# Spreading a gate's weight loads over three units per head pair, and sending DRAM copies one by one between loads

## The chip, the cores and the metric

The kernel runs on one core of one Trainium2 chip. The metric is the device time of one launch in microseconds (us); lower is better. A profiled execution has one more number, its span: the time from the first to the last instruction that the hardware profiler recorded. The core has a matrix engine (PE, with its weight loads shown apart as PEld), a vector engine (DVE), a scalar engine (ACT), a general engine (POOL) and an engine that only issues transfers (SP). Sixteen DMA engines carry the transfers of all of them.

## The reference

The reference is one decoder layer with two branches side by side. Shapes: 512 tokens, width 2048, float32.

```python
cond = jax.nn.silu(c)
mod = cond @ w_ada[layer] + b_ada[layer]
shift, scale, gate = jnp.split(mod, 3, axis=-1)
u = rms_norm(h, norm_w[layer]) * (1.0 + scale[:, None, :]) + shift[:, None, :]
proj = u @ w_in[layer]
z, xbc, dt_raw, q, k, v, g = jnp.split(proj, [OFF_Z, OFF_XBC, OFF_DT, OFF_Q, OFF_K, OFF_V], axis=-1)
...   # SSD branch: conv, chunked scan, gated norm -> y_ssd (2048 wide)
...   # retention branch: 8 heads, rotary q/k, chunkwise recurrence, head norm, silu(g) -> y_ret (2048 wide)
mixed = jnp.concatenate([y_ssd, y_ret], axis=-1) @ w_out[layer]
h = h + gate[:, None, :] * mixed
return rms_norm(h, final_norm_w)
```

The gate is the last third of `cond @ w_ada`: a vector of 2048 numbers made from a 2048 x 2048 block of weights, 16 MB that are read once and used once.

## The kernel before, in words

**Number format.** Every float32 product is made of three TensorE products: an operand is split into a rounded part (`hi`, made by ACT, line 98) and the remainder (`lo`, made by DVE, line 99), and `mm3` (lines 107 to 109) adds hi x hi, hi x lo and lo x hi.

**Units.** The input projection is cut into units of 512 output columns. `unit(name, ...)` walks over the 2048 input rows in 8 steps of 256 rows. A step (`kc`) loads 512 KB into a tile `raw` (SP, line 95), splits it into `hi` and `lo`, and multiplies them into four PSUM banks named `acc` (24 matmuls of 512 columns). The last two steps are multiplied together, bank by bank. `raw` has 3 buffers, `hi` and `lo` 4 each, so SP can issue the load of a step only when the split of the load three places before has been done, and the split waits for PE when four steps lie ready. `unit` has an argument `side`: a function that is called after each step's load is traced.

**Stages.** First the conditioning and a set of units that are built up together. Then the SSD branch, groups 1 to 3, with units BC2, xs1 to xs3 and z1 to z3. Then the retention branch, four head pairs p = 0 to 3, each with a unit qk, a unit v and a unit g. `ret_a` takes the four banks of qk through the rotary step on DVE (lines 474 to 476, tiles `r` and `rt`, then POOL at line 477), `ret_b` runs the chunk recurrence (four chunks; DVE makes statistics of `po` and the new state `rnew` from `pkv`), and `ret_c` multiplies with silu(g) and writes the mixed activations to DRAM through `put_mix`. Last comes the output projection in sweeps over `w_out`, which ends in the gated residual and the norm.

**The gate.** `gate_part(n, q)` loads 512 KB of the gate's weight (block n of 4, eighth q of 8) into a buffer of the same ring `raw` (named `graw`, SP line 577) and adds two row groups into `gacc` with two DVE instructions (line 586 for the first of a block, line 588 for the rest). `gate_done(n)` loads a bias `bg` (line 593), sums over the partitions with one matmul on ones (`pg`, line 595) and adds the bias on DVE (line 596). Before the change the eight parts of block p are issued in unit v of head pair p, one after each load, and `gate_done(p)` follows that unit.

**Sums of the output weight.** The output projection uses 16 row blocks of `w_out`, each with four quarters, and sums of those quarters (T1 to T4). The sums are made by transfers alone, DRAM to DRAM. `block_sums` is called 20 times, at the end of each half stage; its calls are numbered n = 0 to 19. Call n copies the four quarters of block n into T1 to T4 (SP, line 379, 512 KB each; call 14 copies two blocks), and issues accumulating transfers for the blocks n-1, n-2 and n-3 from POOL (line 369). `behind(eng)` puts what follows behind the last instruction of that engine traced so far. The four copies of a call stand one after the other.

**Order of the work.** Each engine runs its own instructions in a fixed order. That order is set when the program is built: a planner simulates the time line and picks among the instructions whose inputs are ready, earlier ones in the program first. It moves instructions of an engine past each other where dependences allow: `bg` of head pair 0 is traced after the unit's loads, and SP issues it before the last two of them.

Of the kernel before, what the change touches and what calls it, by code (L numbers as in the profile page):

```python
# [41 lines left out]
def hybrid_block(ctx, tc, x, c_row, vecs, heads, w_mod, w_gate, b_gate, w_in, w_dt, w_out, fnw,  # L42
                 rope, dmask, xi, zeta, gdec, out):
    nc = tc.nc
    act, dve, pool, pe, sp = nc.scalar, nc.vector, nc.gpsimd, nc.tensor, nc.sync
# [8 lines left out]
    def bank(tag, name):  # L54
        return ps.tile([P, 512], F32, tag=tag, name=name)
# [30 lines left out]
    def hv(base, i):  # L86
        return half[:, base - V_SNW + i:base - V_SNW + i + 1]
# [5 lines left out]
    def load_w(src, width, eng=dve):  # L93
        raw = wp.tile([P, 2, width], F32, tag="raw", bufs=3, name="raw")
        last_load[0] = sp.dma_start(raw.rearrange("p k f -> p (k f)"), src)
        hi = wp.tile([P, 2, width], F32R, tag="hi", bufs=4, name="hi")
        lo = wp.tile([P, 2, width], F32R, tag="lo", bufs=4, name="lo")
        act.copy(hi, raw)  # L98
        eng.tensor_tensor(lo, raw, hi.bitcast(F32), ALU.subtract)  # L99
        return hi, lo  # L100
# [3 lines left out]
    def mm3(dst, a, b, first, last, more=False):  # L104

        (ah, al), (bh, bl) = a, b
        pe.matmul(dst, lhsT=ah, rhs=bh, start=first, stop=False, skip_group_check=more)  # L107
        pe.matmul(dst, lhsT=ah, rhs=bl, start=False, stop=False, skip_group_check=more)  # L108
        pe.matmul(dst, lhsT=al, rhs=bh, start=False, stop=last, skip_group_check=more)  # L109

    def unit(name, w_stationary, tag="mm", side=None):
        width = 512
        nb = width // P if w_stationary else NC
        banks = [bank(tag, f"acc{b}") for b in range(nb)]
        held = []
        for kc in range(NK // 2):
            held.append((kc, *load_w(w_in[name][kc], width)))
            if side is not None:
                side(kc)
            if kc == NK // 2 - 2:  # L120
                continue
            for b in range(nb):
                sl = slice(b * P, (b + 1) * P)
                for k, hi, lo in [(2 * c + kt, h[:, kt, :], l[:, kt, :])
                                  for c, h, l in held for kt in range(2)]:
                    if w_stationary:
                        mm3(banks[b], (hi[:, sl], lo[:, sl]), (uh[k], ul[k]),
                            k == 0, k == NK - 1)
                    else:
                        mm3(banks[b][:, :width], (uh[k][:, sl], ul[k][:, sl]), (hi, lo),  # L130
                            k == 0, k == NK - 1)
            held = []
        return banks
# [158 lines left out]
    def t2k(tag, bufs, name, shape=(P, 512)):  # L292
        pl = att1 if tag in ("bc", "xs", "zs") else att
        return pl.tile(list(shape), F32, tag=tag, bufs=bufs, name=name)
# [27 lines left out]
    B11, B12, B22, B21 = (lambda j, i=i: w_out[4 * j + i] for i in range(4))  # L322
    T1, T2, T3, T4 = (lambda j, i=i: tsum[j][i] for i in range(4))
# [9 lines left out]
    def put_mix(i, src, nw):  # L333


        pT = bank("aux", "pT")
        for c in range(NC):
            pe.transpose(pT[:, c * P:(c + 1) * P], src[c], ident)
        m = t2k("mo", 3, "m")
        act.activation(m, pT, AF.Copy, scale=nw)  # L340
        if i % 2 == 0:
            half_of["m"] = m
            return
        ma, j = half_of["m"], i // 2
        a11, a21, a12, a22 = ma[:, 0:256], ma[:, 256:], m[:, 0:256], m[:, 256:]
        g = t2k("xw", 2, "mg", (P, 2, 256))
        s3 = t2k("xd", 2, "ms", (P, 256))
        pool.tensor_tensor(s3, a11, a21, ALU.subtract)
        pool.tensor_tensor(a21, a21, a22, ALU.subtract)
        pool.tensor_tensor(g[:, 0, :], a21, a11, ALU.subtract)  # L350
        pool.tensor_tensor(g[:, 1, :], a12, g[:, 0, :], ALU.add)
        pool.dma_start(mixd["AS"][j].rearrange("p a t -> p (a t)"), ma)
        pool.dma_start(mixd["SR"][j], g)
        pool.dma_start(mixd["SA"][j][:, 0, :], s3)
        pool.dma_start(mixd["SA"][j][:, 1, :], a12)
        pool.dma_start(mixd["A22"][j // 2][:, j % 2, :], a22)
# [3 lines left out]
    def behind(eng):  # L360

        ins = next(i for i in reversed(nc.cur_bb.bb.instructions) if i.engine == eng.engine)
        return tc.issue_after(ins)

    def block_sums():


        def add(dst, src):
            pool.dma_start(dst, src, accum_op=ALU.add, max_dma_last_dim=4096)

        n = next(ticks)
        for i in range(4):
            for j in {14: (14, 15)}.get(n - i, (n - i,)):
                if not 0 <= j < 2 * QJ or n - i > 14:
                    continue
                if i == 0:
                    with behind(sp):
                        for dst, src in ((T1, B11), (T3, B12), (T2, B22), (T4, B21)):
                            sp.dma_start(dst(j), src(j))
                else:  # L380
                    with behind(pool):
                        if i == 1:
                            add(T1(j), B12(j))
                            add(T3(j), B22(j))
                        elif i == 2:
                            add(T2(j), T1(j))
                        else:
                            add(T4(j), T2(j))
# [62 lines left out]
    def silu2(pb, name, zs=None):  # L451
        th = t2k("th", 2, "th")
        act.activation(th, pb, AF.Tanh, scale=0.5)
        if zs is None:
            zs = t2k("zs", 4, name)
        dve.scalar_tensor_tensor(zs, th, 1.0, pb, ALU.add, ALU.mult)
        return zs
# [99 lines left out]
    def ret_c(p, ys, gb):  # L557
        for c in range(NC):
            gs = silu2(gb[c], f"gs{c}")
            dve.tensor_tensor(ys[c], ys[c], gs, ALU.mult)  # L560
        for i in range(4):
            put_mix(16 + 4 * p + i, [y[:, i * P:(i + 1) * P] for y in ys], hv(V_RNW, 4 * p + i))

    def take_bc(banks, g):
        for j in range(2):
            bct[("B", g + j)] = conv_silu(banks[j], 16 + g + j, "bc", 5, f"B{g + j}")
            bct[("C", g + j)] = conv_silu(banks[2 + j], 20 + g + j, "bc", 5, f"C{g + j}")

    def take_xs(banks, g):
        xst[g] = [conv_silu(b, 4 * g + i, "xs", 5, f"xs{i}") for i, b in enumerate(banks)]  # L570


    gates = {}

    def gate_part(n, q):
        raw = wp.tile([P, 2, 512], F32, tag="raw", bufs=3, name="graw")
        sp.dma_start(raw.rearrange("p k f -> p (k f)"), w_gate[8 * n + q])
        if n % 2 == 0 and q == 0:
            gates["t"] = t2k("dec", 2, "gacc", (P, HPG, P)).rearrange("p (a h) t -> p a (h t)", a=2)
        if q == 0:  # L580
            gates[n] = gates["t"][:, n % 2, :]
        gacc = gates[n]
        for kk in range(2):
            k = 2 * q + kk
            if k == 0:
                dve.tensor_scalar(gacc, raw[:, kk, :], cs[:, k:k + 1], None, ALU.mult)
            else:
                dve.scalar_tensor_tensor(gacc, raw[:, kk, :], cs[:, k:k + 1], gacc,  # L588
                                         ALU.mult, ALU.add)

    def gate_done(n):
        bg = t2k("tmp", 2, "bg")
        sp.dma_start(bg, b_gate[n * 512:(n + 1) * 512].partition_broadcast(P))
        pg = bank("aux", "pg")
        pe.matmul(pg, lhsT=ones, rhs=gates[n], start=True, stop=True)
        dve.tensor_tensor(gates[n], pg, bg, ALU.add)
# [5 lines left out]
    for b in range(4):  # L602
        z = whole("B", b)
# [63 lines left out]
    block_sums()  # L667
    for g in range(1, GROUPS):
        if g == 2:
            take_bc(unit("BC2", True), 2)  # L670
        take_xs(unit(f"xs{g}", True), g)
        ys = ssd_a(g)
        block_sums()
        zb = unit(f"z{g}", False)
        ssd_b(g, ys, [silu2(zb[c], f"zs{c}") for c in range(NC)])
        block_sums()
    for p in range(RH // 2):
        qk = unit(f"qk{p}", True)
        a = ret_a(p, qk)
        block_sums()  # L680
        vb = unit(f"v{p}", False, side=lambda kc: gate_part(p, kc))
        gate_done(p)
        ys = ret_b(p, a, vb)
        block_sums()
        gb = unit(f"g{p}", False)
        ret_c(p, ys, gb)
        block_sums()


# [229 lines left out]
```

## Time and profile before

| what | value |
|---|---|
| time of three runs | 1493.32, 1495.53, 1495.69 us (median 1495.53) |
| the profiled execution | 1496.37 us, span 1494.7 us |
| mean granted TensorE clock | 0.987 |
| PE busy | 1438.2 us, 96% of the span |
| DVE busy | 895.1 us, 60% |
| ACT busy | 540.2 us, 36% |
| POOL busy | 377.2 us, 25% |
| bytes moved by DMA | 324.09 MB, mean 217 GB/s |

The page of the profile gives busy time by engine, the span in 40 slices, the chain of work that ended last, the costliest groups of instructions, and the issues of transfers with the time from issue to landing. Two things help to read it. A matmul's recorded duration (0.39 us) is longer than the distance to the next one (0.23 us) because matmuls are pipelined, so short pauses of PE hide behind a busy share near 100%; the count of matmuls in a stretch of time shows them better. And a wait is written as "who waited <- for whom", with the idle time.

### The profile page before, as it was taken

To read this page: it belongs to the slowest core of one execution; us is meant where nothing else is said; L and a number is where in the kernel's file an instruction comes from. 1 tells how busy PE (TensorE), PEld (TensorE's weight loads), DVE (VectorE), ACT (ScalarE), POOL (GpSimd) and SP (SyncE) were. 2 spreads that over 40 slices of the span, in tenths; PEclk is the share of its full clock that TensorE was granted. 3 is DMA by queue.
4 is the path that set the end of the run, shared out by engine and by line. 5 is a ranking of instruction groups with operands and counts; after the bars stand their busy time and mean duration, and the time that the engine had idled before them with its cause. 6 is when DMAs were issued, how large, how long until landed. Compare 5 with 4: busy or idle time off the path is not lost.

```text
span 1494.7 us, 17196 instructions
## 1 busy us (share of the span) xinstructions
PE 1438.2 (96%) x6481; PEld 1174.4 (79%) x6481; DVE 895.1 (60%) x1064; ACT 540.2 (36%) x732; POOL 377.2 (25%) x440
## 2 busy tenths in 40 slices
PE   6998999899999999999999999999899999999997
PEld 4766888788888888778877888888788778888885
DVE  6899786777556654643363436433644466558585
ACT  7423353434424423121312131213232356446453
POOL 4540105576035245301340124023200200000000
PEclk9999999999999999999999999999999999999999
DMA  9887753556647748876578659664744598777755
GB/s 361 339 316 282 246 185 99 185 161 185 212 160 199 216 155 239 217 255 189 189 202 258 181 184 285 213 158 136 207 155 143 190 320 279 246 244 263 245 179 195
DMA packets 86263, 324.09 MB, mean 217 GB/s; under 512 B 11298, under 2 KB 11474, under 8 KB 81058
## 3 DMA queue, kind: packets, MB, share of 16 engines
q1 hardware_dynamic: 67858, 262.30, 51.2%
q0 software_dynamic: 17168, 58.59, 16.9%
q10 hardware_dynamic: 1152, 2.10, 0.4%
q8 instruction: 51, 0.84, 0.2%
q14 instruction: 34, 0.27, 0.1%
HBM read 304.00 MB, written 86.05 MB: 261 GB/s over the span
## 4 chain that ended last, share of the span: by engine, by line
PE 64%; DVE 13%; DMA 10%; issue 8%; POOL 3%; ACT 1%; SPq 1%; DVEq 0%; POOLq 0%; ACTq 0%
PE acc L108 13%; PE acc L107 13%; PE acc L109 13%; DMA graw<-w_gate_d 5%; DVE ada L189 4%; PE U L108 3%; PE U L109 3%; PE U L107 3%; PE W L107 2%; PE W L108 2%; PE W L109 2%; DVE gacc L588 1%; DVE lo L99 1%; PE py L428 1%; DVE ul L206 1%
## 5 line engine op out<-in xcount | busy, mean ns | idle before, releaser
L98 ACT CAST hi<-raw 128x1024 fp32r<-128x1024 f32 (+1 forms) x184 | 186.1, 1015 | 483.5 <-PE acc L109 150.6
L99 DVE TENSOR_TENSOR lo<-raw,hi 128x1024 fp32r<-128x1024 f32 (+1 forms) x166 | 210.5, 1271 | 250.0 <-ACT hi L98 249.6
L107 PE MATMUL acc<-hi,uh 128*128 128x512 f32 x704 | 278.2, 397 | 8.9 <-DVE rt L476 6.4
L108 PE MATMUL acc<-lo,uh 128*128 128x512 f32 x704 | 280.5, 398 | 1.6 <-DVE lo L99 1.5
L109 PE MATMUL acc<-hi,ul 128*128 128x512 f32 x704 | 278.4, 396 | 0.0
L108 PE MATMUL acc<-ul,hi 128*128 128x512 f32 x512 | 200.5, 392 | 0.0
L109 PE MATMUL acc<-uh,lo 128*128 128x512 f32 x512 | 200.1, 391 | 0.0
L107 PE MATMUL acc<-uh,hi 128*128 128x512 f32 x512 | 199.8, 392 | 0.0
L752 DVE TENSOR_TENSOR lo<-raw,hi 128x1024 fp32r<-128x1024 f32 x112 | 137.2, 1231 | 83.0 <-ACT hi L751 82.9
L107 PEld LDWEIGHTS acc<-hi,uh 128*128 128x128 f32 x704 | 133.6, 190 | 40.1 <-DVE rt L476 7.1
L751 ACT CAST hi<-raw 128x1024 fp32r<-128x1024 f32 x112 | 117.6, 1053 | 129.5 <-PE W L109 53.5
L108 PEld LDWEIGHTS acc<-lo,uh 128*128 128x128 f32 x704 | 133.8, 190 | 30.5 <-DVE lo L99 3.0
L109 PEld LDWEIGHTS acc<-hi,ul 128*128 128x128 f32 x704 | 133.4, 189 | 27.9 <-issue 0.5
L107 PEld LDWEIGHTS acc<-uh,hi 128*128 128x128 f32 x512 | 96.2, 188 | 19.5
L108 PEld LDWEIGHTS acc<-ul,hi 128*128 128x128 f32 x512 | 96.2, 188 | 19.5
L109 PEld LDWEIGHTS acc<-uh,lo 128*128 128x128 f32 x512 | 96.2, 188 | 19.3
L108 PE MATMUL U<-lo,mh 128*128 128x512 f32 x256 | 99.9, 390 | 0.8 <-DVE lo L752 0.8
L109 PE MATMUL U<-hi,ml 128*128 128x512 f32 x256 | 99.7, 390 | 0.0
L588 DVE SCALAR_TENSOR_TENSOR gacc<-graw,cs,gacc 128x512 f32<-128x512 f32 x60 | 54.2, 904 | 73.2 <-DMA graw<-w_gate_d 72.1
L107 PE MATMUL U<-hi,mh 128*128 128x512 f32 x256 | 95.2, 390 | 0.0
L189 DVE SCALAR_TENSOR_TENSOR ada<-ada,csb 128x2048 f32<-128x2048 f32 x32 | 91.0, 2846 | 0.3 <-DMA ada<-w_mod_d 0.3
L108 PE MATMUL W<-lo,mh 128*128 128x512 f32 x192 | 75.6, 394 | 0.1
(244 smaller groups left out, 2170.7 us busy)
## 6 DMA issues: line engine op xcount, KB each, us to landing
ada<-w_mod_d SPq DMA_DIRECT2D x32, 1024.0 KB, 6.2
T<-w_out_d SPq DMA_DIRECT2D x64, 512.0 KB, 7.8
raw<-T SPq DMA_DIRECT2D x64, 512.0 KB, 4.3
raw<-w_out_d SPq DMA_DIRECT2D x48, 512.0 KB, 4.3
raw<-w_in_z SPq DMA_DIRECT2D x32, 512.0 KB, 4.8
T<-w_out_d POOLq DMA_DIRECT2D x32, 512.0 KB, 8.8
T<-T POOLq DMA_DIRECT2D x32, 512.0 KB, 13.6
raw<-w_in_qk SPq DMA_DIRECT2D x32, 512.0 KB, 4.2
```

The lines of the kernel that those rows point to most:

```text
L98: act.copy(hi, raw)
L99: eng.tensor_tensor(lo, raw, hi.bitcast(F32), ALU.subtract)
L107: pe.matmul(dst, lhsT=ah, rhs=bh, start=first, stop=False, skip_group_check=more)
L108: pe.matmul(dst, lhsT=ah, rhs=bl, start=False, stop=False, skip_group_check=more)
L109: pe.matmul(dst, lhsT=al, rhs=bh, start=False, stop=last, skip_group_check=more)
L189: dve.scalar_tensor_tensor(ada, ada, 0.5, csb, ALU.mult, ALU.mult, accum_out=dst)
L206: dve.tensor_tensor(l_k, xT[k], h_k.bitcast(F32), ALU.subtract)
L428: pe.matmul(py[:, hd], lhsT=dec[:, h, :], rhs=xd[:, hd], start=True, stop=True)
L588: dve.scalar_tensor_tensor(gacc, raw[:, kk, :], cs[:, k:k + 1], gacc, ALU.mult, ALU.add)
L751: act.copy(dst[0], src)
L752: dve.tensor_tensor(dst[1], src, dst[0].bitcast(F32), ALU.subtract)
```

## The change

The change has three parts.

1. The gate's parts are issued through `between`, which is called after every load of the units qk, v and g: 96 calls in all. Every third call (the second, fifth, ...) issues one gate part, the others send one copy if one is queued. So a head pair's eight parts lie in its three units, 3 in qk, 2 in v and 3 in g. `gate_done(p)` moves from behind unit v to behind `ret_c(p)`.
2. `block_sums` no longer issues the four copies of its block. It puts them in a list, `copies`. In the SSD units `trickle` sends one after every second load, in the retention units `between` sends them.
3. What is left in the list at the next call of `block_sums` is sent there, ahead of the accumulating transfers. Nothing is copied or added more or less often than before.

```diff
+    copies = []
+
+    def copy_one():
+        if copies:
+            with behind(sp):
+                sp.dma_start(*copies.pop(0))
+
+    def trickle(kc):
+        if kc % 2:
+            copy_one()
+
     def block_sums():
...
         n = next(ticks)
+        while copies:
+            copy_one()
         for i in range(4):
...
                 if i == 0:
-                    with behind(sp):
-                        for dst, src in ((T1, B11), (T3, B12), (T2, B22), (T4, B21)):
-                            sp.dma_start(dst(j), src(j))
+                    copies.extend((dst(j), src(j)) for dst, src in
+                                  ((T1, B11), (T3, B12), (T2, B22), (T4, B21)))
...
+    turns = iter(range(1000))
+
+    def between(kc):
+        i = next(turns)
+        if i % 3 == 1:
+            gate_part(i // 24, i // 3 % 8)
+        else:
+            copy_one()
+
...
-            take_bc(unit("BC2", True), 2)
-        take_xs(unit(f"xs{g}", True), g)
+            take_bc(unit("BC2", True, side=trickle), 2)
+        take_xs(unit(f"xs{g}", True, side=trickle), g)
         ys = ssd_a(g)
         block_sums()
-        zb = unit(f"z{g}", False)
+        zb = unit(f"z{g}", False, side=trickle)
...
-        qk = unit(f"qk{p}", True)
+        qk = unit(f"qk{p}", True, side=between)
         a = ret_a(p, qk)
         block_sums()
-        vb = unit(f"v{p}", False, side=lambda kc: gate_part(p, kc))
-        gate_done(p)
+        vb = unit(f"v{p}", False, side=between)
         ys = ret_b(p, a, vb)
         block_sums()
-        gb = unit(f"g{p}", False)
+        gb = unit(f"g{p}", False, side=between)
         ret_c(p, ys, gb)
+        gate_done(p)
         block_sums()
```

## The prediction

> **What bounds the kernel now.** I read the page first, then busy time by stretches of time, then PE's time line where those show a hole, then the waits and the chain of waits for what made it.
>
> ```profile
> span 1494.7 us, 17196 instructions
> ```
>
> PE's busy time in chosen stretches, matmul counts in brackets. The first row is of the view for all engines (PE first, then PEld, DVE, ACT, POOL), the others for PE alone, each 12 us long. The last three columns are clock, DMA share and GB/s.
>
> ```profile
> 400.00:500.00 100.00, 100.00 (x485) 82.18 (x484) 59.25 (x64) 37.93 (x54) 44.11 (x54) 1.00 0.60 185
> ```
>
> ```profile
> 500.00:512.00 12.00, 12.00 (x56) 1.00 0.86 227
> 612.00:624.00 12.00, 10.64 (x47) 1.00 0.54 159
> 653.00:665.00 12.00, 10.03 (x36) 0.86 0.78 249
> 764.00:776.00 12.00, 8.81 (x37) 1.00 0.39 133
> 804.00:816.00 12.00, 9.91 (x34) 0.86 0.75 221
> 914.00:926.00 12.00, 12.00 (x54) 1.00 0.95 255
> 1062.00:1074.00 12.00, 10.13 (x44) 1.00 0.44 113
> 1074.00:1086.00 12.00, 9.21 (x47) 0.86 0.79 227
> ```
>
> PE bounds the kernel: in the SSD stage (400 to 500) it never pauses, and 56 matmuls fit into 12 us (500 to 512), 0.214 us each by this count. Nothing that leaves PE's work alone can gain there. All that the change can win lies in the holes, and those stand in the unit v of head pair 0 (612 and 653), of pair 1 (764 and 804) and of pair 3 (1062 and 1074). Pair 2 has none (914 to 926: 54). Matmuls short of 56: 9 + 20 + 19 + 22 + 12 = 82, times 0.214 = 17.6 us. The last stretch holds short transposes, so I take its idle time, 12.00 - 9.21 = 2.8. Together **20.4 us**. Now what made them; PE's time line, the wait in square brackets:
>
> ```profile
> 619.18 0.50 PE L107 MATMUL acc<-hi,uh 128*128 128x512 f32 x1 [1.36 <-DVE rt L476]
> ...
> 656.24 0.51 PE L107 MATMUL acc<-hi,uh 128*128 128x512 f32 x1 [1.21 <-ACT hi L98]
> ...
> 659.35 0.63 PE L107 MATMUL acc<-hi,uh 128*128 128x512 f32 x1
> 659.77 0.63 PE L108 MATMUL acc<-lo,uh 128*128 128x512 f32 x1
> ...
> 1078.58 0.90 PE L491 MATMUL pk<-ident,r 128*128 128x128 f32 x3 [2.79 <-POOL r L477]
> ```
>
> There are two kinds. At 619, 764 and 1062 to 1086 unit v cannot start in a bank before DVE has taken the bank of qk through the rotary step: DVE is late. At 656 and 809 the next weights are not there: the ring has run dry. Dry holes cost 20 + 22 matmuls, 9.0 us; rotary holes the other 11.4. Behind a dry hole matmuls come every 0.42 us (659.35, 659.77) with a granted clock of 0.86 over the stretch; this tail is in the 20 and the 22. Both kinds lead to the gate's weight. The waits:
>
> ```profile
> DVE gacc L588 <- DMA graw<-w_gate_d: 72.1, 19, 10.1
> ...
> DVE gacc L586 <- DMA graw<-w_gate_d: 12.3, 3, 7.3
> ```
>
> DVE stood still for 84.4 us because a gate part had not landed, with `lo` and rotary instructions queued behind it. The same by unit v, pairs 0 to 3 (the view of tile graw in four windows):
>
> ```profile
>   DMA graw<-w_gate_d: 21.5, 5
> ```
> ```profile
>   DMA graw<-w_gate_d: 31.6, 6
> ```
> ```profile
>   DMA graw<-w_gate_d: 7.7, 4
> ```
> ```profile
>   DMA graw<-w_gate_d: 23.5, 7
> ```
>
> The pair with 7.7 us of such waits is the pair without holes. The chain of waits and SP's time line show the two longest waits, each right behind four copies, and the one of pair 3, which has no copies near:
>
> ```profile
> 635.03 14.85 DMA graw<-w_gate_d
> ...
> 786.91 16.18 DMA graw<-w_gate_d
> ...
> 1047.58 10.11 DMA graw<-w_gate_d
> ```
>
> ```profile
> 631.74 3.19 SPq L379 DMA_DIRECT2D T<-w_out_d  x4
> ...
> 784.42 2.39 SPq L379 DMA_DIRECT2D T<-w_out_d  x4
> ```
>
> **The change part by part.** Transfers, median time from issue to landing in the last column:
>
> ```profile
> T<-w_out_d SPq DMA_DIRECT2D x64, 512.0 KB, 7.8
> ...
> T<-w_out_d POOLq DMA_DIRECT2D x32, 512.0 KB, 8.8
> T<-T POOLq DMA_DIRECT2D x32, 512.0 KB, 13.6
> raw<-w_in_qk SPq DMA_DIRECT2D x32, 512.0 KB, 4.2
> raw<-w_in_v SPq DMA_DIRECT2D x32, 512.0 KB, 7.8
> graw<-w_gate_d SPq DMA_DIRECT2D x32, 512.0 KB, 4.7
> ```
>
> *Copies one by one.* The 64 copies stay, with their bytes. At most one stands between two loads, where four (once eight) stood. What a load waits behind four is the 14.85 and 16.18 above against a median of 4.7: some 11 us, 2.7 for each copy. So a load loses at most about 2.7 us now, and the ring, seven steps deep, can bear that. I take both dry holes as filled: **-9.0 us**. Bounds: 0 (the accumulating transfers alone keep the ring late) to -9.0. On SP a copy takes 2.39 / 4 = 0.6 us to issue, and SP has that time, since it waits for the ring:
>
> ```profile
> SPq L95 <- DVE lo L99: 629.0, 127, 38.9
> ```
>
> In the SSD units the change is worth nothing either way: PE has no hole there, and cover is the same ring. Call 14 leaves 8 copies for the 6 free turns of v2; two are sent at call 15 right ahead of the accumulating transfers. If POOL then has to wait for a copy (7.8 us), the rotary additions on POOL stand behind it, and the nearest price of a late one is the 2.79 us above. Bounds 0 and +2.8; I take 0, since call 15 is traced behind `ret_b`, a unit's length after most of its copies.
>
> *Gate parts 3, 2, 3 instead of 0, 8, 0.* DVE's work is the same. In unit v the ring carries 10 loads instead of 16, and DVE waits for 2 parts instead of 8, so the rotary holes should shrink. But qk and g, which had no gate part, have 24 now, and each can hold up DVE. Price of one: at best 1.0 us (pair 2, 7.7 over 8 parts), at worst 3.9 (pair 1, 31.6 over 8); 2.9 in pair 3, where no copies stood near. I take 2.0, since copies no longer bunch but the accumulating transfers do. A wait costs PE something only if it falls into a change of units, where DVE has to free banks or carry a recurrence: a stretch of 12 us as in the rows above, of a unit of 192 x 0.214 = 41 us and some chunk work: a quarter, so 8 of the 32 parts, 16 us of waits. Before, the rotary holes cost 11.4 us in the three bad pairs, whose waits sum to 76.6 us; no row splits these by place, and I put half, 38, into the change of units: 0.30 us of PE for each us of such a wait. So 16 x 0.30 = 4.8 us of rotary-like holes remain or arise: -11.4 + 4.8 = **-6.6 us**. Bounds: -11.4 (no wait matters) and +14 (all 24 new parts at 2.0 x 0.30, on top of unchanged holes).
>
> *`gate_done` behind `ret_c`.* The groups of the lines view, mean ns after the bar:
>
> ```profile
> L595 PE MATMUL pg<-gacc,ones 128*128 128x512 f32 x8 | 4.1, 592 | 0.0
> ...
> L596 DVE TENSOR_TENSOR gacc<-pg,bg 128x512 f32<-128x512 f32 x4 | 2.8, 692 | 0.0
> ...
> L693 ACT COPY gate<-gacc 128x512 f32<-128x512 f32 x4 | 2.4, 619 | 0.4 <-PE psc L497 0.4
> ```
>
> About 1.0 us of PE, 0.7 of DVE and 0.6 of ACT per pair move, and none is new. For pairs 0 to 2 nothing waits for them. For pair 3 they now fall into the start of the output projection, together with a fifth user of the four auxiliary PSUM banks ahead of it: between -1 (they leave the start of `ret_b`) and +2. I take 0; the first gate is used sweeps later.
>
> **Sum:** -9.0 - 6.6 = -15.6 us. The profiled execution took 1496.37 us (span 1494.7, so 1.7 lie around it) and stands 0.8 above the median of 1495.53. 1496.4 - 15.6 = 1480.8, or 1479.9 from the median: **1480**.
>
> One rule bears on the tails. The Trainium skill, TensorE: Matmul & The Clock Gate, section "What's actually happening", says that the clock halves after an idle window of about 3.4 us and comes back after as long a busy one. The half pace agrees with the 0.42 us spacing, but here PE waited only 1.21 us and then a little more before it slowed. By the page alone such short holes would carry no slow tail, and the tails, about 4 us of the 20.4, would have to be counted as something that the change does not cure: 1484.
>
> **The rivals.**
>
> *Accumulating transfers are the cause (1491).* POOL's transfers take 8.8 and 13.6 us, come four at a time and stay as they are. Pair 3 has no copies and still lost 12 matmuls and 2.8 us. For it: graw at 1047.58 took 10.11 us with POOL's transfers alone in the way. Against it: the two dry holes, the deepest, stand behind copies. Then only half of the dry holes goes (-4.5) and the rotary holes move about but keep their sum: 1495.5 - 4.5 = 1491; with the dry holes kept as well, no change. The Trainium skill, DMA: Bandwidth & Descriptors, section "Issuing engines are not separate DMA queues", says that transfers of all issuing engines interleave on the same 16 DMA engines; so copies that are merely spread still meet POOL's, which speaks for this rival.
>
> *The recurrence in unit g waits for gate parts (1504, slower).* In `ret_b` a chunk's state comes back to PE through DVE, and PE's order leaves little room. The chain of waits of pair 0:
>
> ```profile
> 674.69 0.87 PE pkv L546 x4
> 678.89 0.86 PE pkv L546 x4
> ```
>
> A step each 4.2 us. A gate part of unit g that lands late now stops DVE in it, which could not happen before, and PE stops at once. Twelve parts fall into the g units; at 2.9 us (pair 3) it is up to 35 us in a place where each counts. It decides once more than 20.4 / 2.9 = 7 of the 12 hit a step. With 10 of them 29 us are lost against 20.4 won: 1495.5 + 8.6 = 1504. Against it: loads run several steps ahead of PE, so most of g's parts land before `ret_b` starts.
>
> *The planner undoes it (1495).* The order on SP is picked from a simulated time line; if it bunches the copies again and puts DVE's gate parts where they were, nothing changes.
>
> **How the numbers follow.** Forecast, most holes gone (1472 to 1488): 0.50. More than all holes, since later stages fall better too (below 1472): 0.05. Accumulating transfers (1488 to 1495): 0.20, two thirds of it faster by over 0.2%. Planner: 0.05. Recurrence or another new wait on DVE (1499 to 1510): 0.20. A difference of 0.2%, 3 us, is about what a measurement of this kernel tells from none (the three runs span 2.4 us). Faster: 0.50 + 0.05 + 0.12 = 0.67; same: 0.08 + 0.05 = 0.13; slower: 0.20. The range that leaves out no more than two in ten runs from 1470 to 1501; the forecast's own is 1472 to 1488.
>
> **What the profile after would show.** Right: DVE's wait for graw well under 84.4 us; graw's longest landing below 10 us where 14.85 and 16.18 stood; ACT's waits for w_in_v gone; unit v free of holes at its end, and stretches of retention with 54 to 56 matmuls in 12 us. Wrong: PE waits at `po` or `pkv` on DVE `rnew`, or new waits on `rt` or `hi` in qk and g; a bunch of four copies in SP's time line; POOL waiting for T. The prediction fails most likely through the 2.0 us per gate part or through the 0.30 us that each us of wait costs: both are shares that no row of this profile gives directly.

## The result, and the profile after

The changed kernel takes 1472.32 us (median of four runs, 1471.68 to 1472.55) against 1494.42 us (median of four, 1491.97 to 1495.69) before: a ratio of 0.9857, 95% interval 0.984 to 0.9875, or 22.1 us less. The profiled execution went from 1496.37 to 1472.30 us, 24.1 us less. The forecast was 1480, 15.6 us less, with a range from 1470 to 1501.

The page after, first lines:

```profile
span 1470.6 us, 17174 instructions
PE 1429.3 (97%) x6481; PEld 1167.7 (79%) x6481; DVE 889.3 (60%) x1064; ACT 540.5 (37%) x732; POOL 385.2 (26%) x440
```

PE has the same 6481 matmuls. To see where the time came from, take two landmarks on PE's time line: the last `po` of the SSD branch, and the short stall in the first sweep of the output projection. Before:

```profile
562.04 0.65 PE L432 MATMUL po<-new,C 128*128 128x512 f32 x1
```
```profile
1193.83 0.72 PE L107 MATMUL W<-hi,mh 128*128 128x512 f32 x1 [1.86 <-ACT m L340]
```

After:

```profile
560.19 0.65 PE L445 MATMUL po<-new,C 128*128 128x512 f32 x1
```
```profile
1170.98 0.50 PE L107 MATMUL W<-hi,mh 128*128 128x512 f32 x1 [1.37 <-ACT m L340]
```

1.9 us are won up to the first landmark, 21.0 between the two, which is the retention stage, and 1.2 behind the second. So 21.0 of the 24.1 us lie in the stage where the prediction saw the holes (20.4 us by its count). Busy time of PE in 12 us stretches after; they answer to the stretches from 612, 653, 764, 804 and 1062 of before, placed at the same spots of head pairs 0, 0, 1, 1 and 3:

```profile
610.00:622.00 12.00, 12.00 (x55) 1.00 1.02 306
...
644.00:656.00 12.00, 12.00 (x54) 1.00 0.73 256
750.00:762.00 12.00, 12.00 (x55) 1.00 0.76 296
790.00:802.00 12.00, 12.00 (x54) 1.00 0.69 253
...
1054.00:1066.00 12.00, 12.00 (x66) 1.00 0.65 194
```

Where 47, 36, 37, 34 and 44 matmuls stood there are 54 or more (the last stretch holds short transposes too), and the granted clock is 1.00, also in the two where it was 0.86. What PE waited for from 530 to 1150, first before, then after:

```profile
PE acc L107 <- DVE rt L476: 6.4, 6, 2.3
PE pk L491 <- POOL r L477: 2.8, 1, 2.8
PE acc L107 <- ACT hi L98: 2.4, 2, 1.2
PE acc L108 <- DVE lo L99: 1.5, 2, 0.8
```
```profile
PE pT L338 <- DVE y L479: 0.8, 1, 0.8
```

The first two lines of before are the rotary holes, the next two the dry ones. All four are gone. (These figures count a pause only beyond a matmul's modelled end, so they are smaller than the loss by counted matmuls.) Transfers after:

```profile
T<-w_out_d SPq DMA_DIRECT2D x64, 512.0 KB, 5.2
...
T<-w_out_d POOLq DMA_DIRECT2D x32, 512.0 KB, 8.3
T<-T POOLq DMA_DIRECT2D x32, 512.0 KB, 14.6
...
graw<-w_gate_d SPq DMA_DIRECT2D x32, 512.0 KB, 4.4
```

The copies land in 5.2 us instead of 7.8. The gate parts, least, median and most from issue to landing:

```profile
DMA to landing us min/median/max: 3.3/4.4/9.5
```

The longest was 16.2 us before. ACT's waits for the weights of unit v, before and then after:

```profile
ACT hi L98 <- DMA raw<-w_in_v: 126.0, 21, 13.1
```
```profile
ACT hi L98 <- DMA raw<-w_in_v: 32.4, 6, 6.9
```

They are a quarter of what they were; the prediction had them gone. But one row went the wrong way. DVE's waits for gate parts:

```profile
DVE gacc L612 <- DMA graw<-w_gate_d: 85.9, 28, 7.4
...
DVE gacc L610 <- DMA graw<-w_gate_d: 24.8, 3, 8.7
```

110.7 us, where 84.4 stood before. DVE stands still for gate parts longer than it did, and PE does not mind. DVE's time line at the change from qk to v of head pair 0 shows why. Before, then after; the wait is in square brackets:

```profile
609.56 0.75 DVE L588 SCALAR_TENSOR_TENSOR gacc<-graw,cs,gacc 128x512 f32<-128x512 f32 x1 [7.30 <-DMA graw<-w_gate_d]
610.23 1.22 DVE L99 TENSOR_TENSOR lo<-raw,hi 128x1024 fp32r<-128x1024 f32 x1
611.37 0.75 DVE L588 SCALAR_TENSOR_TENSOR gacc<-graw,cs,gacc 128x512 f32<-128x512 f32 x1
612.03 0.68 DVE L474 TENSOR_TENSOR r<-acc,cosb 128x512 f32<-128x512 f32 x1
```
```profile
608.96 0.68 DVE L489 TENSOR_TENSOR rt<-acc,sinb 64x512 f32<-64x512 f32 x1
610.42 1.15 DVE L612 SCALAR_TENSOR_TENSOR gacc<-graw,cs,gacc 128x512 f32<-128x512 f32 x1 [0.78 <-DMA graw<-w_gate_d]
611.49 0.68 DVE L487 TENSOR_TENSOR r<-acc,cosb 128x512 f32<-128x512 f32 x1
```

Before, a wait of 7.30 us stood right ahead of the first bank's rotary step. After, one gate part falls between two banks, with a wait of 0.78 us. The long waits lie elsewhere, and behind nearly all of them stood nothing that PE needed soon. The exception is a wait of 5.04 us that ends at 578: the next instruction of DVE makes `y`, a tile of the SSD branch, and PE pauses 0.8 us for it, its only pause in this stretch.

### The profile page after: what moved, and what is told of

The parts are those of the page before. It is cut to its first block, busy times and chain, and to the rows that moved or that the text cites. A ratio compares the mean times of both kernels' runs of the same rounds, so it can differ in the third digit from the quotient of the medians.

```text
span 1470.6 us, 17174 instructions
## 1 busy us (share of the span) xinstructions
PE 1429.3 (97%) x6481; PEld 1167.7 (79%) x6481; DVE 889.3 (60%) x1064; ACT 540.5 (37%) x732; POOL 385.2 (26%) x440
## 4 chain that ended last, share of the span: by engine, by line
PE 71%; DVE 11%; issue 8%; DMA 5%; POOL 3%; ACT 1%; SPq 0%; DVEq 0%; POOLq 0%; ACTq 0%
PE acc L109 16%; PE acc L108 16%; PE acc L107 16%; DVE ada L189 5%; PE U L108 3%; PE U L109 3%; PE U L107 3%; PE W L107 2%; PE W L109 2%; PE W L108 2%; DVE ul L206 1%; PE py L441 1%; DVE lo L99 1%; PE po L538 1%; DMA ada<-w_mod_d 1%
## 5 line engine op out<-in xcount | busy, mean ns | idle before, releaser
L99 DVE TENSOR_TENSOR lo<-raw,hi 128x1024 fp32r<-128x1024 f32 (+1 forms) x166 | 215.9, 1307 | 212.3 <-ACT hi L98 211.7
L108 PE MATMUL acc<-lo,uh 128*128 128x512 f32 x704 | 276.7, 393 | 0.6 <-DVE lo L99 0.6
L109 PE MATMUL acc<-hi,ul 128*128 128x512 f32 x704 | 274.6, 391 | 0.0
L612 DVE SCALAR_TENSOR_TENSOR gacc<-graw,cs,gacc 128x512 f32<-128x512 f32 x60 | 47.9, 798 | 86.7 <-DMA graw<-w_gate_d 85.9
```

## The experiments

All times are medians. The kernel before ran beside each of the three groups of experiments (1, 2, 3 and 4; 5 to 8; 9 to 11) and took 1493.6 to 1493.9 us there; ratios and gains are against those runs. PE's waits are those from 530 to 1150 us.

**1. Gate parts spread, copies four at a time.**

```diff
-                    copies.extend((dst(j), src(j)) for dst, src in
-                                  ((T1, B11), (T3, B12), (T2, B22), (T4, B21)))
+                    with behind(sp):
+                        for dst, src in ((T1, B11), (T3, B12), (T2, B22), (T4, B21)):
+                            sp.dma_start(dst(j), src(j))
```
(against the kernel after)

> The kernel after the change, but the four copies of a call again stand one after the other on SP; the gate parts stay spread 3, 2, 3. The prediction's own split (copies made the dry holes, 9.0 us; gate parts in unit v made the rotary holes, 11.4 us): 1494 - 11 = about 1482, with two dry holes left. Ring theory (what hurts is two loads per step through a ring of three buffers; with 10 or 11 loads per unit a landing of 15 us now and then is borne): 1472 to 1476, no holes in retention. Copies theory (bunched copies are the whole cause): 1488 or more.

1476.41 us, ratio 0.9878 (0.9859 to 0.9898): 17.5 us of the 22. PE's waits, then the copies of call 14 on SP:

```profile
PE acc L107 <- DVE rt L490: 1.8, 2, 1.4
PE pT L338 <- DVE y L480: 0.7, 1, 0.7
```
```profile
875.68 5.46 SPq L393 DMA_DIRECT2D T<-w_out_d  x8
```

The dry holes are gone although copies bunch as before; the prediction's split (1482, two dry holes left) is refuted, and the ring theory's 1472 to 1476 is met within half a microsecond. The waits for `rt` that are left stand at 906 to 910, in the pair whose v unit starts behind eight copies.

**2. Copies one by one, gate parts all in v.**

```diff
-        qk = unit(f"qk{p}", True, side=between)
+        qk = unit(f"qk{p}", True, side=trickle)
...
-        vb = unit(f"v{p}", False, side=between)
+        vb = unit(f"v{p}", False, side=lambda kc: (gate_part(p, kc), trickle(kc)))
+        gate_done(p)
...
-        gb = unit(f"g{p}", False, side=between)
+        gb = unit(f"g{p}", False, side=trickle)
         ret_c(p, ys, gb)
-        gate_done(p)
```
(against the kernel after)

> The kernel before the change, but copies are sent one after every second load, in all units; all eight gate parts stay in unit v, one per load. The prediction's split: 1494 - 9 = about 1485, rotary holes left. Ring theory: unit v still carries 16 loads (and four copies) through three buffers, so most holes stay: 1487 to 1494. Copies theory: 1472 to 1476.

1489.51 us, ratio 0.9976 (0.9954 to 0.9998): 4.4 us, more than nothing only by a hair. It lies in the ring theory's range. PE's waits:

```profile
PE acc L107 <- DVE rt L489: 6.1, 6, 1.8
PE pk L504 <- POOL r L490: 3.4, 1, 3.4
PE acc L108 <- DVE lo L99: 1.3, 2, 0.7
```

Here too the dry holes have shrunk, from the 3.9 us of both lines before to 1.3, and the rotary holes are as they were. So the deep dry holes came where 16 loads in one unit met a bunch of copies in front, and either part of the change cures most of them. (Experiment 6 shows a third condition, the accumulating transfers.) Of the two parts only the spreading cures the rotary holes. The two parts' gains, 17.5 and 4.4, add up to the 22 of the change within their intervals.

**3 and 4. All eight parts in qk, or all in g** (copies by `trickle`, `gate_done` behind `ret_c`), to tell place from density.

```diff
+        qk = unit(f"qk{p}", True, side=lambda kc: (gate_part(p, kc), trickle(kc)))   # experiment 3
+        vb = unit(f"v{p}", False, side=trickle)
+        gb = unit(f"g{p}", False, side=trickle)
```
```diff
+        qk = unit(f"qk{p}", True, side=trickle)                                      # experiment 4
+        vb = unit(f"v{p}", False, side=trickle)
+        gb = unit(f"g{p}", False, side=lambda kc: (gate_part(p, kc), trickle(kc)))
```
(the lines that replace those with `between` in the kernel after)

> Copies one after every second load; all eight gate parts of a head pair in unit qk, one per load, none in v and g. If the place counts (gate parts must not stand where DVE frees the banks of qk through the rotary step): 1472 to 1477. Ring theory: the holes move with the 16 loads, to the end of unit qk and its change to v, and stay about as large: 1484 to 1492.

> Copies one after every second load; all eight gate parts in unit g, one per load, none in qk and v. If the place counts: 1472 to 1477. Ring theory: holes at the end of unit g, 1484 to 1492. The rival of the prediction (DVE, stopped by a late gate part, holds up the chunk recurrence of the pair, which runs beside unit g): slower than with the parts in qk, 1495 or more, with PE waits at po or pkv.

In qk: 1488.51 us, ratio 0.9961 (0.994 to 0.9982). In g: 1475.31 us, 0.987 (0.9852 to 0.9888). Equal density, 13 us apart, so the place counts. PE's waits, in qk first (a fifth line, 0.6 us for `y` at `pT`, is left out):

```profile
PE pT L338 <- DVE yr L573: 6.3, 5, 2.1
PE acc L109 <- DVE lo L99: 3.0, 1, 3.0
PE pT L338 <- DVE y L479: 2.0, 1, 2.0
PE acc L107 <- DVE rt L489: 1.7, 2, 1.3
```
```profile
PE po L540 <- DVE rnew L565: 2.9, 3, 1.5
```

With the parts in qk, DVE's stops fall on the silu(g) products of the pair before (`yr`, line 573 there), and PE waits for them at `pT`. DVE's time line of that kernel at one such place:

```profile
717.75 1.54 DVE L612 SCALAR_TENSOR_TENSOR gacc<-graw,cs,gacc 128x512 f32<-128x512 f32 x2 [3.37 <-DMA graw<-w_gate_d]
719.21 0.68 DVE L469 SCALAR_TENSOR_TENSOR gs<-th,acc 128x512 f32<-128x512 f32 x1
719.92 0.69 DVE L573 TENSOR_TENSOR yr<-yr,gs 128x512 f32<-128x512 f32 x1
```

I had tied the theory of place to the rotary steps alone and so expected qk to be harmless; that was too narrow. Units v and qk both have such a place, where DVE owes PE something soon. The ring has its share in qk too: the time lies in the ring theory's range, and the 3.0 us for `lo` stand at the end of unit qk of pair 0, where that theory had them. But 8.9 of the 13.6 us of pauses are waits at `pT`, and in g, at the same density, the ring theory's 1484 to 1492 fails. With the parts in g the prediction's rival shows up, PE waiting at `po` for `rnew`, but in three pauses of 2.9 us together, where the prediction had up to 35.

**5. `gate_done` behind `ret_c`, alone.**

```diff
-        gate_done(p)
         ys = ret_b(p, a, vb)
...
         ret_c(p, ys, gb)
+        gate_done(p)
```
(against the kernel before)

> The kernel before, with only gate_done moved from behind unit v to behind ret_c. Prediction: nothing, 1491 to 1497; the holes of unit v unchanged. If the move itself were part of the gain (it takes a matmul, a DVE addition and a wait for the last gate part out of the start of the recurrence): 1488 to 1491.

1494.53 us, ratio 1.0009 (0.9996 to 1.0022): nothing.

**6. The kernel before without the accumulating transfers.**

```diff
-            pool.dma_start(dst, src, accum_op=ALU.add, max_dma_last_dim=4096)
+            return
```

> The kernel before without POOL's accumulating transfers; the sums T1 to T4 are then plain copies, so this leaves out part of the computation. If late landings are what turns gate parts into holes, most of which stand behind POOL's four transfers: gate parts land in 4 to 6 us, holes of retention mostly gone, 1472 to 1478. If it is the mere presence of gate arithmetic among the rotary steps on DVE (1.5 us a part): holes stay, 1488 or more.

1481.01 us, ratio 0.9918 (0.9903 to 0.9932): 12.6 us, less than expected. In the retention stage the profile shows more: from the last `po` of the SSD branch (562.67) to the stall in the first sweep (1175.96) it takes 613.3 us, where the kernel before took 631.8 and the kernel after 610.8. The stretches ahead of it and behind it are 2.8 us longer than before. ACT's waits for w_in_v fell from 126.0 to 22.9 us. PE's waits:

```profile
PE acc L107 <- DVE rt L476: 1.6, 1, 1.6
PE pk L491 <- POOL r L477: 0.7, 1, 0.7
```

So 18.5 of the 21.0 us of the retention stage go without POOL's transfers, with every gate part still in v and the copies still in fours: what turned most gate parts into holes were their late landings (the median of all 32 fell from 4.7 to 3.7 us, the longest from 16.2 to 11.5). One rotary hole is left, in pair 3, where every gate part lands within 4.7 us; there the parts stand between the rotary steps of DVE without being late.

**7. The kernel before, gate arithmetic on POOL.**

```diff
-                dve.scalar_tensor_tensor(gacc, raw[:, kk, :], cs[:, k:k + 1], gacc,
-                                         ALU.mult, ALU.add)
+                pool.tensor_scalar(raw[:, kk, :], raw[:, kk, :], cs[:, k:k + 1], None, ALU.mult)
+                pool.tensor_tensor(gacc, raw[:, kk, :], gacc, ALU.add)
```
(and the first part's multiply on POOL)

> The kernel before, with the gate's multiply and add on POOL instead of DVE (three POOL instructions for two DVE ones); loads, ring and places unchanged. If rotary holes come from DVE standing still for a gate part that has not landed: waits of DVE for rt gone from PE's list, dry holes left, 1481 to 1486. If they come from the ring that carries 16 loads: holes as before, 1492 or more. POOL also adds the rotary halves and could now be late itself: then PE waits for POOL r at pk, 1490 or more.

1521.97 us, ratio 1.0192 (1.0177 to 1.0208): 28 us slower. Only the open ends of the last two cases (1492 or more, 1490 or more) cover that, and neither case had its reason: the holes are not as before, and PE has no wait for POOL `r`. But PE's waits separate the two kinds of hole:

```profile
PE acc L107 <- ACT hi L98: 24.5, 13, 6.8
PE acc L108 <- DVE lo L99: 4.5, 5, 1.2
```

With the gate off DVE, no wait for `rt` is left: the rotary holes were DVE's stops. And the dry holes grew. POOL needs two instructions of 1.57 and 1.30 us where DVE needed one of 0.75, so it gives the ring's buffers back later; that fits the ring as the cause of dry holes.

**8. The kernel before, gate parts in buffers of their own** (256 KB each, four idle silu tiles), so that the ring carries 8 loads in v.

```diff
-        raw = wp.tile([P, 2, 512], F32, tag="raw", bufs=3, name="graw")
-        sp.dma_start(raw.rearrange("p k f -> p (k f)"), w_gate[8 * n + q])
+        raw = [t2k("zs", 4, "graw") for _ in range(2)]
+        for kk in range(2):
+            sp.dma_start(raw[kk], w_gate[8 * n + q][:, kk * 512:(kk + 1) * 512])
```

> The kernel before, with the gate's loads in four buffers of 256 KB that are idle in unit v (those of the silu tiles), in 64 loads of half the size, so that the ring raw carries unit v's 8 loads alone; DVE's arithmetic and its places unchanged. If the ring is the cause of the dry holes: ACT's waits for w_in_v shrink from 126 us to under 40, dry holes gone, rotary holes left, 1483 to 1487. If DVE's stops alone make all holes: 1491 or more. If the ring makes all: 1474 to 1478.

1491.09 us, ratio 0.9989 (0.9974 to 1.0005): not told from no change. PE's waits:

```profile
PE acc L107 <- DVE rt L476: 7.9, 4, 4.4
PE acc L109 <- DVE lo L99: 2.2, 1, 2.2
```

The waits of `acc` for ACT `hi`, the sign of a dry hole, are gone; one wait for `lo` is left, at 607, the end of unit qk. ACT's waits for w_in_v fell to 55.7 us. Rotary waits are no smaller, one of them 4.4 us long. In its waits this is the mirror image of experiment 7. Its time is not: it falls where DVE's stops alone were to make all holes (1491 or more), and 55.7 us missed the "under 40". The change was not a clean one: gate parts landed later than before (median 5.8 us for half the size, longest 18.5), and the rotary holes that follow are deeper, with a granted clock of 0.86 behind two of them. So how much of the loss the dry holes were is not shown by this run.

**9. The kernel after, gate arithmetic on POOL** (the swap of experiment 7).

> The kernel after the change, with the gate's multiply and add on POOL instead of DVE, as in the kernel before with the same swap (1522 us, dry holes in units v and g, no wait for rt). If the dry holes there came from 16 loads in one unit through a ring that POOL frees late, they shrink with 10 or 11 loads per unit: 1472 to 1485. If POOL is too slow to free the ring at any density: 1500 or more. DVE's 110.7 us of waits for gate parts are gone either way: should the time be clearly below 1472, those waits did cost something after the change; if not, they were idle time.

1478.16 us, ratio 0.9893 (0.9878 to 0.9908). The same swap cost 28 us before the change and costs about 6 after it; no wait for ACT `hi` is left in the stretch:

```profile
PE pk L504 <- POOL r L490: 1.7, 3, 1.0
PE acc L107 <- DVE rt L489: 1.2, 1, 1.2
```

With 10 or 11 loads per unit the ring bears a consumer that frees it late. The time is not below 1472 although 110.7 us of waits are off DVE; since POOL's lateness costs something of its own here, that alone does not show that those waits were free. Experiment 11 is the clearer case.

**10. Parts 4, 0, 4 instead of 3, 2, 3.**

```diff
-        if i % 3 == 1:
-            gate_part(i // 24, i // 3 % 8)
+        p, at = divmod(i, 24)
+        if at // 8 != 1 and at % 2:
+            gate_part(p, at // 2 if at < 8 else at // 2 - 4)
```
(against the kernel after)

> The kernel after the change, with the eight parts 4, 0, 4 over qk, v and g instead of 3, 2, 3, the copies in the other turns. If what counts is that few gate parts meet the rotary steps on DVE, and two in v are few enough: within 3 us of the kernel after (1470 to 1475). If the two parts in v still cost: 1465 to 1469. If density in qk and g rises to where it hurts (one part to two loads): 1476 to 1480, with waits of PE for pT or po.

1476.1 us, ratio 0.9876 (0.986 to 0.9893), where the kernel after has 0.9857 (0.984 to 0.9875) from its own runs. PE's waits are 1.0 us for `yr` at `pT` and 0.7 for `rt`. That is 1 us beyond the first case and at the near end of the third (density), but the two intervals overlap, so it is not told from the kernel after. It is no better, so there is no sign that the two parts in v cost anything; a small gain in v could hide behind a small loss in qk and g.

**11. The kernel after without the accumulating transfers** (the cut of experiment 6).

> The kernel after the change without POOL's accumulating transfers (T1 to T4 are then plain copies; part of the computation is left out). The same cut took 12.4 us from the kernel before. If the change cured what those transfers cause: within 3 us of the kernel after, 1469 to 1473. If they still cost something there: 1460 to 1468, and spreading them would be worth a try.

1474.04 us, ratio 0.9866 (0.9852 to 0.9881). That is 1 us above the first range. What took 12.6 us from the kernel before takes nothing from the kernel after. PE has no wait in the stretch at all. The tile graw in this kernel, DVE's idle time and the landings (least, median, most):

```profile
  DMA graw<-w_gate_d: 84.3, 29
...
DMA to landing us min/median/max: 3.2/3.5/4.3
```

Every gate part lands within 4.3 us and DVE still "waits" 84.3 us for them: here that is idle time with a name on it, not a cost.

## Why the prediction was right, and where not

*The bound and the place.* PE bounds the kernel, the retention stage holds all the loss, and the change returns it: right, 21.0 us between the landmarks against 20.4 counted as holes. That the two are so close is in part chance. The count took 56 matmuls in 12 us for the full pace, but the last of the 56 are short ones: from 500.06 to 511.62 the matmuls of 512 columns come every 0.227 us, and 53 of them fit. Against 53 the five stretches lack 67 matmuls, 15.2 us, and with the 2.8 us that makes 18.0.

*Copies, -9.0.* Wrong in the attribution. Alone they give 4.4 us (experiment 2), and the dry holes close without them as well (experiment 1). The rows quoted, a gate part landing after 14.85 and 16.18 us right behind four copies, were true, but they told which load was late and not that it was enough to empty the ring: that took a unit with 16 loads. Nor were the 11 us the copies' alone, 2.7 for each: one by one, with POOL's transfers in place, the longest landing is still 13.7 us (experiment 2), and in fours, without POOL's transfers, 11.5 (experiment 6). The step that failed is reading a hole's last cause as its only one.

*Gate parts, -11.4 + 4.8.* The -11.4 came; the +4.8 did not. That term was 16 us of waits at 0.30 us of PE for each, and both factors fail: DVE's waits grew to 110.7 us, and what is left for PE in the stretch is one pause of 0.8 us, though that one does stand behind a new part in qk, as the term had it. No fixed price per us of wait fits these runs: waits of 84.3 us went with no pause of PE at all (experiment 11), 142.6 with 1.7 (experiment 10), 84.4 with 13.1 (the kernel before). What counts is what stands behind a wait on DVE. This mis-sized term makes about 4 of the 8.5 us by which the profiled execution beat the sum (24.1 against 15.6). Of the rest, 1.9 and 1.2 us stand outside retention, and no run shows that they come from the change: in experiments 2 to 4, whose SSD units are those of the kernel after, the first landmark lies at 560.0 to 562.5 us, and the stretch behind the second takes 299.2 us in experiment 5, which has the copies and gate parts of the kernel before, and 299.6 in the kernel after.

*The sum.* It came out near with terms that were not. Alone, the copies gave 4.4 us where the sum has 9.0, and the spreading 17.5 where it has 6.6; both were made together, so the wrong split did not show in the time. The 1472.32 us lie only 0.3 us inside the forecast's own range, 1472 to 1488.

*`gate_done`, 0.* Right (experiment 5).

*SSD units, 0.* Right: the 1.9 us at the first landmark lie within the 2.5 us by which kernels with the same SSD units differ there.

*Rivals.* The accumulating transfers are a cause, worth 12.6 us before and 18.5 in the retention stage (experiment 6), so the rival's premise was right. But they are one as a partner: spreading the parts makes them harmless (experiment 11), and so the rival's 1491 failed. The recurrence rival is real as a mechanism, 2.9 us of pauses with all eight parts in g (experiment 4), and far too dear as priced; whether that is because loads run ahead of PE, as the argument against it said, no run shows. The planner kept the copies apart, but for three in a row at 922 us, and PE has no pause there.

*The signs.* Right: graw's longest landing, 9.5 us; full stretches in unit v; no wait of PE for `rnew`, `rt` or `hi` in retention. Nearly right: ACT's waits for w_in_v, 32.4 us left. Not right: DVE's wait for graw, named as a sign of success if it fell well under 84.4 us, rose to 110.7.

*The clock.* The slow tails went with the holes; the granted clock in the stretches is 1.00. So they were rightly counted as part of what the change cures, and the reading by the rule of the Trainium skill (TensorE: Matmul & The Clock Gate, section "What's actually happening"), which left them out and gave 1484, does not hold here: the last section has the rows.

## What to carry to other kernels

A load that feeds side work should not share a small buffer ring and an engine that runs its instructions in order with the main stream just where that engine owes the bottleneck something; spread it thin, or put it where the engine is free (here unit g, within 3 us of the spread, and not qk, 16 us off). Judge a wait by what is queued behind it on its engine and who needs that, never by its sum: here the sum rose by 26 us while the time fell by 22. When two bursts meet, thinning either one may be enough, so take the parts apart before crediting one of them.

## What the runs showed of the hardware

Short pauses were enough to slow PE, but not every time. In the kernel before, the pause of 1.21 us at 656 was followed by a second one:

```profile
657.50 0.50 PE L108 MATMUL acc<-lo,uh 128*128 128x512 f32 x1 [0.75 <-DVE lo L99]
657.83 0.44 PE L109 MATMUL acc<-hi,ul 128*128 128x512 f32 x1
658.07 0.63 PE L107 MATMUL acc<-hi,uh 128*128 128x512 f32 x1
```

From 658.07 to 661.48 matmuls then came every 0.42 us. A pause of 1.36 us at 619 left the pace at 0.23 us and the granted clock of its stretch at 1.00, and so did three pauses of 0.70, 2.27 and 0.22 us between 767 and 775. In experiment 2 a pause of 1.80 us at 627, six microseconds after one of 0.64, was followed by half pace again. So neither the length of a pause nor their number tells here when the slow stretch comes; what does stays open.

The accumulating transfers that POOL issues can slow the loads that SP issues. In the kernel before w_in_v landed after a median of 7.8 us; without them, in experiment 6, with the same loads in the same units:

```profile
raw<-w_in_v SPq DMA_DIRECT2D x32, 512.0 KB, 4.2
```

Not all loads felt it: w_in_g, in the next unit, landed after 4.2 us in both.
